# The opening of a hybrid attention layer: the inverse rms spread inside the value products, and the forget gates' turn, sum and store made steps of the planned list

## The chip, the cores and the metric

One core of a Trainium2 chip runs the whole layer. Its engines are TensorE (PE, matrix products into PSUM), VectorE (DVE), ScalarE (ACT), GpSimd (POOL) and SyncE (SP, which here issues all DMAs). Each takes its instructions in order from its own queue and waits on semaphores for the others. The metric is the device time of one execution in microseconds.

## What is computed

One layer with sequence 1024 and width 1024: a combined projection feeds two head groups, each of 8 heads of 64; their output is normalised and projected; then a cross-attention to 256 memory tokens and a squared-ReLU MLP follow. Only the start of it matters here:

```python
h = rmsnorm(x, g_mix_pre[l])
proj = h @ w_in[l]
...
f_logit = proj[..., o0:o0 + FOX_HEADS] + b_fgt[l]
...
# forgetting_attention
logf = jax.nn.log_sigmoid(f_logit.astype(jnp.float32))
c = jnp.cumsum(logf, axis=1).transpose(0, 2, 1)
...
logits = logits + c[:, :, q0:q1, None] - c[:, :, None, :q1]
```

So the first head group needs, beside q, k and v, the running sum c of the log forget gates over the sequence, for 8 heads.

## The kernel before

**Products.** Every float32 operand is split into a high part (a rounded copy, made by ScalarE) and a low part (the difference, made by VectorE or GpSimd), and `mm3` makes a product out of three passes: high by high, high by low, low by high (lines 174 to 176).

**Order.** The opening is written out by hand, lines 1422 to 1493: each engine gets its instructions in the order of the calls. Behind it `attention_phase` (line 1282) runs a planner, `Flow`. It takes steps for TensorE from seven streams by priority (values, turns of the probabilities, scores, side steps, two streams of row statistics, projections as filler). A step has a cost and a condition, and work that it leaves for the other engines goes into lists: "V" VectorE, "S" ScalarE, "G" GpSimd, "D" the DMA queue of SP, each with a start time, a cost and a level (lower goes first). The planner's clock starts at 0 with the phase, and `flow.free` says from when it takes an engine to be free. What it plans fixes the order of each queue; on the chip the semaphores decide the times.

**The opening.** x is there transposed, in two halves of 512 positions (`xf[0]`, `xf[1]`), each with 8 blocks of 128 features (kc). The values of the first group are made from x times the gain only, and scaled by the inverse rms afterwards, so they needn't wait for the norm:

- `plain_split(th, kc)` splits x times gain of half th into `hT[th]` (lines 1362 and 1363).
- `value_part(banks, th, w, kcs)` multiplies those kc into four PSUM banks. V is the first group of 256 value columns, with the 8 gate columns beside them, W the second 256. V uses the banks with tags "mm" and "s", W those with "tr" and "pv"; each tag has two buffers.
- `square(b)` sums the squares of a block of 128 positions (ScalarE, line 1369); `root(th)` makes the inverse rms of a half on GpSimd (lines 1375 and 1376) and four diagonal matrices from it on VectorE (line 1379).
- `values_out` copies the banks out, scaled by the inverse rms: ScalarE the high part (line 1416) and the gate column (line 1418), VectorE the low part (line 1419).
- `spread(th, d, tag)` multiplies a matrix of ones with the diagonals, which lays the inverse rms along the free axis (TensorE, line 1384), and copies it out (ScalarE, line 1386).
- `norm(th, kc)` scales x by gain and inverse rms in place (VectorE, line 1391), and `norm_split(th, kc)` splits the result into `hT[th]` again (lines 1396 and 1397), now for q and k.
- `forget_gates` gives the log sigmoid of the gates as a list of eleven small steps (`gparts`, lines 381 to 394, with an Exp, a Ln and an Exp on ScalarE, lines 387, 389 and 391), the turn (8 transposes on TensorE, line 399, and two copies, line 400), the running sum (a memset and a scan on VectorE, lines 403 and 404), and the store to DRAM (line 406). The bias tiles of the first head group are read back from there, spread over 128 partitions (line 433).
- `stock.split_now(2)` splits the first weights of q and k: ScalarE the high parts (line 311), GpSimd the low parts in halves (line 320).
- `bias_rows` prepares the relative biases of the second group (lines 223 to 228).

**The start of the phase.** The projections of the first pair of heads come as filler in the order q, k of the first half, q, k of the second, 8 steps of 0.681 us each, and their copies (lines 697 and 698 for q, 704 to 706 for k). The first scores (lines 495 and 496) need q and k of both halves and the bias tile. A side step needs a PSUM buffer of tag "tr".

Of the kernel before, what the change touches and what calls it, by code (L numbers as in the profile page):

```python
# [17 lines left out]
AF = mybir.ActivationFunctionType  # L18
# [4 lines left out]
P = 128  # L23
S = 1024
D = 1024
# [110 lines left out]
def build(ctx, tc, nc, out, t):  # L136
# [13 lines left out]
    def mm_tile(shape, name, tag="mm"):  # L150
        return psp.tile(shape, F32, tag=tag, bufs=2, name=name)
# [224 lines left out]
    def forget_gates():  # L376

        z, e, l, u = [p1.tile([P, TB, 8], F32, tag="fg", bufs=4, name=f"f{n}") for n in "zelu"]
        ea, la, ua = [p1.tile([8, S], F32, tag="klo", bufs=4, name=f"f{n}a") for n in "elu"]
        vec, act = nc.vector, nc.scalar  # L380
        calls = [lambda b=b: vec.tensor_add(z[:, b, :], fcol[:, b, :], bfgt) for b in range(TB)]
        rows_ = lambda: [calls.pop(0)() for _ in range(TB)]
        parts = [
            rows_,
            lambda: vec.tensor_scalar(l, z, -1.0, None, op0=ALU.mult),
            lambda: vec.tensor_tensor(l, l, z, op=ALU.min),
            lambda: act.activation(e, l, AF.Exp),
            lambda: vec.tensor_scalar(u, e, 1.0, None, op0=ALU.add),
            lambda: act.activation(l, u, AF.Ln),
            lambda: vec.scalar_tensor_tensor(e, u, 1.0, e, op0=ALU.subtract, op1=ALU.subtract),  # L390
            lambda: act.activation(u, l, AF.Exp, scale=-1.0),
            lambda: vec.tensor_tensor(e, e, u, op=ALU.mult),
            lambda: vec.tensor_sub(e, e, l),
            lambda: vec.scalar_tensor_tensor(e, z, 0.0, e, op0=ALU.min, op1=ALU.add)]

        def turn(g):
            tr = mm_tile([8, 4, P], f"ftr{g}", "s")
            for j in range(4):
                nc.tensor.transpose(tr[:, j, :], e[:, g * 4 + j, :], ident)
            act.activation(ea[:, g * HT:(g + 1) * HT], tr.rearrange("p a b -> p (a b)"), AF.Copy)  # L400

        def scan():
            vec.memset(ua, 0.0)
            vec.tensor_tensor_scan(la, ea, ua, 0.0, op0=ALU.add, op1=ALU.add)

        return parts, turn, scan, lambda: nc.sync.dma_start(cd, la)

    bias, qs, kd, kl, vs2, probs, trs, pvs = {}, {}, {}, {}, {}, {}, {}, {}
    heads = [(n, a) for n in range(8) for a in range(2)]
# [308 lines left out]

    def side_steps():

        for n in range(4, 8):
            for th in range(2):
                yield 0.436, lambda: there(("vt", n, th)) and free["tr"].ready()
                free["tr"].take()
                tr = mm_tile([P, 4, P], f"vtr{n}{th}", "tr")
                for b in range(4):
                    nc.tensor.transpose(tr[:, b, :], vt[n][:, th * HT + b * P:th * HT + (b + 1) * P], ident)
                src = tr.rearrange("p b (a d) -> p b a d", d=64)
                dst = vs2[n][th]

                def lo(at, src=src, dst=dst, key=("v", n, th)):
                    flow.put("V", at, 0.7, lambda: nc.vector.tensor_sub(
                        dst[:, :, :, 64:128], src, f(dst[:, :, :, 0:64])),
                        lambda end: (free["tr"].give(end), seen.__setitem__(key, end)), 1)

                flow.put("S", flow.end, 0.6, lambda src=src, dst=dst: nc.scalar.activation(
                    dst[:, :, :, 0:64], src, AF.Copy), lo, 1)
            free["u4"].give(flow.end)
        mT = Act("mT", NM)
        mem_in.append(mT)  # L740
        for k in range(0, KC, 2):
            yield 0.436, lambda: there("mem") and free["tr"].ready() and (k or free["u4"].ready(4))
            free["tr"].take()
            if k == 0:
                for _ in range(4):
                    free["u4"].take()
            tr = mm_tile([P, 2, 2, P], f"tr_mem{k}", "tr")
            for j in range(2):
                for q in range(2):
                    nc.tensor.transpose(tr[:, j, q, :], mem_in[q][:, (k + j) * P:(k + j + 1) * P], ident)  # L750
            src = tr.rearrange("p a q b -> p a (q b)")
            i, o = k // mT.per, k % mT.per
            dh, dl = mT.h[i][:, o:o + 2, :], mT.l[i][:, o:o + 2, :]

            def lo(at, src=src, dh=dh, dl=dl, k=k):
                flow.put("V", at, 0.7, lambda: nc.vector.tensor_sub(dl, src, f(dh)),
                         lambda end: (free["tr"].give(end), seen.__setitem__(("mT", k), end)), 1)

            flow.put("S", flow.end, 0.6, lambda src=src, dh=dh: nc.scalar.activation(dh, src, AF.Copy), lo, 1)
        for _ in range(2):  # L760
            free["raw"].give(flow.end)
# [534 lines left out]
    with tc.manual_schedule():  # L1296
# [76 lines left out]
        def root(th):  # L1373
            r = rall[:, th * 4:th * 4 + 4]
            nc.gpsimd.tensor_scalar(r, ssx[th], EPS, None, op0=ALU.add)
            nc.gpsimd.tensor_tensor(r, r, mhalf[:, 0:4], op=ALU.pow)
            d = p1.tile([P, 4, P], F32, tag="ph", bufs=2, name=f"diag{th}")
            for b in range(4):
                nc.vector.tensor_scalar(d[:, b, :], ident, r[:, b:b + 1], 1.0, op0=ALU.mult, op1=ALU.mult)
            return d  # L1380

        def spread(th, d, tag):
            ps = mm_tile([P, HT], f"rt{th}", tag)
            nc.tensor.matmul(ps, ones, d.rearrange("p a b -> p (a b)"), start=True, stop=True)
            r = p1.tile([P, HT], F32, tag="pl", bufs=2, name=f"rt{th}")
            nc.scalar.activation(r, ps, AF.Copy)
            rt.append(r)
# [16 lines left out]
        def value_part(banks, th, w, kcs):  # L1404
            for kc in kcs:
                for b in range(4):
                    c = slice(b * P, (b + 1) * P)
                    mm3(banks[b], hT[th].hi(kc, c), hT[th].lo(kc, c), *w[kc], kc == 0, kc == KC - 1)

        def values_out(g, th, banks):  # L1410
            for b in range(4):
                kb = th * 4 + b
                r = rall[:, kb:kb + 1]
                src = banks[b][:, 0:256].rearrange("p (h d) -> p h d", d=64)
                dh = vs[g][kb // 2][:, kb % 2, :, 0:64]
                nc.scalar.activation(dh, src, AF.Copy, scale=r)
                if g == 0:
                    nc.scalar.activation(fcol[:, kb, :], banks[b][:, 256:264], AF.Copy, scale=r)
                nc.vector.scalar_tensor_tensor(vs[g][kb // 2][:, kb % 2, :, 64:128], src, r, f(dh),
                                               op0=ALU.mult, op1=ALU.subtract)  # L1420
# [21 lines left out]
        nc.sync.dma_start(gcol, t["g_heads"])  # L1442
        stock.load(3)
        W = value_banks(1, 0)
        value_part(W, 0, w1, range(KC))
        d = root(0)
        values_out(0, 0, V)
        for kc in range(8):
            plain_split(1, kc)
        V = value_banks(0, 1)  # L1450
        value_part(V, 1, w0, range(4))
        values_out(1, 0, W)
        spread(0, d, "pv")
        value_part(V, 1, w0, range(4, 8))
        for b in range(4, 8):
            square(b)
        for kc in range(KC):
            norm(0, kc)
        d = root(1)
        for kc in range(KC):  # L1460
            norm_split(0, kc)
        W = value_banks(1, 1)
        value_part(W, 1, w1, range(3))
        gparts, turn, scan, gate_store = forget_gates()
        values_out(0, 1, V)
        spread(1, d, "s")
        value_part(W, 1, w1, range(3, 6))
        for call in gparts[:4]:
            call()
        stock.split_now(2)  # L1470
        for kc in range(4):
            norm(1, kc)
        for call in gparts[4:6]:
            call()
        for kc in range(4, KC):
            norm(1, kc)
        for call in gparts[6:]:
            call()
        for g in range(2):
            turn(g)  # L1480
        value_part(W, 1, w1, range(6, 8))
        for kc in range(4):
            norm_split(1, kc)
        scan()
        for kc in range(4, KC):
            norm_split(1, kc)
        values_out(1, 1, W)
        bias_rows(0)
        bias_rows(1)
        seen["gates"] = 11.0  # L1490
        flow.put("D", 7.0, 0.55, gate_store, None, -1)
        flow.put("D", 14.0, 0.55, lambda: nc.sync.dma_start(rd, rows[0]))
        flow.free.update(V=7.0, S=4.0)
        km, vmh, vml = attention_phase()
    p1s.close()

# [666 lines left out]
```

## Time and profile before

| | us |
|---|---|
| median of 3 runs | 1500.74 |
| lowest and highest run | 1495.99, 1501.56 |
| the profiled execution | 1498.95 |
| its span, first to last instruction | 1497.2 |

| engine | busy us | share of the span | instructions |
|---|---|---|---|
| TensorE | 1468.1 | 98% | 7564 |
| VectorE | 926.4 | 62% | 1599 |
| ScalarE | 794.6 | 53% | 1426 |
| GpSimd | 374.6 | 25% | 464 |

How to read the rows below. A row of a timeline has the start in us, the time it takes in us, the engine, the line of the kernel, the operation, what it writes and reads, the shape, and how many instructions are put together; in brackets stands how long the engine had been idle and what ended that. With several instructions, the time is from the first start to the last end. A row of the list of waits has who waited for whom, the total in us, how often, and the longest. A row of windows has the stretch, its length, the busy time of the engine, the granted TensorE clock (1.00 is full), the share of the DMA engines and GB/s.

### The profile page before, as it was taken

What the parts mean: (1) busy time and instruction counts of PE and PEld (TensorE: products, weight loads), DVE (VectorE), ACT (ScalarE), POOL (GpSimd) and SP (SyncE); (2) the same over time, 40 slices, a digit from 0 to 9 for tenths busy, and PEclk for the clock granted to TensorE, in tenths of its full rate; (3) what the DMA queues carried; (4) which work ended last, traced back from release to release, by engine and by line L of the source; (5) the groups of instructions that cost most, each with busy time, mean ns of one, the idle gap of its engine ahead of it and who ended that gap; (6) DMA issues with size and microseconds to landing.
All of it is one profiled execution on the core that took longest, in us unless ns stands there. A gap on an engine that the chain in (4) does not pass through costs nothing. (4 is left out here: it accounts for less than half of the span.)

```text
span 1497.2 us, 21427 instructions
## 1 busy us (share of the span) xinstructions
PE 1468.1 (98%) x7564; PEld 1250.3 (84%) x7564; DVE 926.4 (62%) x1599; ACT 794.6 (53%) x1426; POOL 374.6 (25%) x464
## 2 busy tenths in 40 slices
PE   8799999999999999999999999999999999999998
PEld 8678888888889988888888887888888888888886
DVE  4757766655565764884374577775545674646577
ACT  6537766666666763463354445555555553444442
POOL 1225444434333310431031422333323000000021
PEclk9899999999999999999999999999999999999999
DMA  8023222534225468461251356774345685436475
GB/s 325 29 86 103 68 77 66 157 94 137 75 76 153 140 249 300 173 236 58 76 178 57 103 182 201 259 247 145 139 161 176 231 343 203 140 121 212 174 253 197
DMA packets 95355, 239.54 MB, mean 160 GB/s; under 512 B 11896, under 2 KB 20224, under 8 KB 95248
## 3 DMA queue, kind: packets, MB, share of 16 engines
q1 hardware_dynamic: 95248, 238.18, 47.3%
q8 instruction: 59, 0.97, 0.3%
q14 instruction: 48, 0.39, 0.1%
HBM read 170.45 MB, written 59.30 MB: 153 GB/s over the span
## 5 line engine op out<-in xcount | busy, mean ns | idle before, releaser
L574 DVE TENSOR_TENSOR pl<-ptr,ph 128x512 fp32r<-128x512 f32 (+1 forms) x152 | 92.3, 615 | 63.1 <-ACT ph L577 62.6
L577 ACT ACTIVATE ph<-ptr 128x512 fp32r<-128x512 f32 (+1 forms) x152 | 79.6, 539 | 48.8 <-PE ptr L568 44.3
L1887 ACT ACTIVATE whif<-ra 128x1024 fp32r<-128x1024 f32 x37 | 39.2, 1060 | 122.7 <-PE fy L175 62.6
L1889 DVE TENSOR_TENSOR wlof<-ra,whif 128x1024 fp32r<-128x1024 f32 x37 | 45.3, 1225 | 91.3 <-ACT whif L1887 91.2
L2003 POOL TENSOR_SCALAR rf<-sf 128x1 f32<-128x1 f32 x8 | 8.2, 1030 | 326.3 <-ACT jf L1988 326.0
L174 PE MATMUL fx<-vhif,whif 128*128 128x512 f32 x168 | 65.4, 389 | 0.0
L176 PE MATMUL fx<-vhif,wlof 128*128 128x512 f32 x168 | 65.4, 389 | 0.0
L175 PE MATMUL fx<-vlof,whif 128*128 128x512 f32 x168 | 65.4, 389 | 0.0
L608 PE MATMUL pv<-pl,vs 128*128 128x256 f32 (+1 forms) x304 | 64.6, 294 | 0.2 <-DVE pl L574 0.2
L608 PEld LDWEIGHTS pv<-ph,vs 128*128 128x128 f32 x304 | 53.1, 189 | 7.3
L608 PE MATMUL pv<-ph,vs 128*128 128x256 f32 (+1 forms) x304 | 58.1, 272 | 0.0
L1777 POOL TENSOR_TENSOR sc<-wf,wf 128x512 f32<-128x512 f32 x14 | 21.9, 1565 | 143.6 <-DMA wf<-in_w_ff 87.7
L174 PE MATMUL k<-hT_hi,whik 128*128 128x512 f32 x128 | 52.2, 408 | 0.0
L174 PE MATMUL mq<-h2T_hi,whimq 128*128 128x512 f32 x128 | 51.6, 403 | 0.0
L174 PE MATMUL yw<-whiwo,yT_hi 128*128 128x512 f32 x128 | 50.8, 397 | 0.6 <-ACT yt L1047 0.6
L174 PE MATMUL q<-hT_hi,whiq 128*128 128x512 f32 x128 | 51.0, 399 | 0.4 <-DVE qs L698 0.4
L174 PE MATMUL ym<-whimo,oT_hi 128*128 128x512 f32 x128 | 50.3, 394 | 0.1
L175 PE MATMUL q<-hT_lo,whiq 128*128 128x512 f32 x128 | 50.1, 392 | 0.0
L175 PE MATMUL k<-hT_lo,whik 128*128 128x512 f32 x128 | 50.1, 391 | 0.0
L176 PE MATMUL k<-hT_hi,wlok 128*128 128x512 f32 x128 | 50.1, 391 | 0.0
L176 PE MATMUL q<-hT_hi,wloq 128*128 128x512 f32 x128 | 50.1, 391 | 0.0
L175 PE MATMUL mq<-h2T_lo,whimq 128*128 128x512 f32 x128 | 50.0, 391 | 0.0
(597 smaller groups left out, 4987.8 us busy)
## 6 DMA issues: line engine op xcount, KB each, us to landing
ra<-gd SPq DMA_DIRECT2D x56, 512.0 KB, 3.6
wg<-in_w_ff SPq DMA_DIRECT2D x56, 512.0 KB, 5.0
wf<-in_w_ff SPq DMA_DIRECT2D x38, 512.0 KB, 4.0
gd<-s SPq DMA_DIRECT2D x48, 256.0 KB, 2.1
wrawmq<-in_w_mq SPq DMA_DIRECT2D x16, 512.0 KB, 3.7
wrawmo<-in_w_mo SPq DMA_DIRECT2D x16, 512.0 KB, 3.9
gd<-u SPq DMA_DIRECT2D x32, 256.0 KB, 2.1
gd<-g SPq DMA_DIRECT2D x25, 256.0 KB, 2.5
```

Source lines behind the costliest of these rows:

```text
L174: nc.tensor.matmul(ps, lh, rh, start=start, stop=False, skip_group_check=more)
L175: nc.tensor.matmul(ps, lh, rl, start=False, stop=False, skip_group_check=more)
L176: nc.tensor.matmul(ps, ll, rh, start=False, stop=stop, skip_group_check=more)
L574: flow.put("V", at, 0.56 if dead else 0.7, lambda: nc.vector.tensor_sub(pl[:, live, :], tr[:, live, :], f(ph[:, live, :])), done)
L577: flow.put("S", flow.end, 0.49 if dead else 0.6, lambda ph=ph, tr=tr, live=live: nc.scalar.activation(ph[:, live, :], tr[:, live, :], AF.C ...
L608: nc.tensor.matmul(pv[:, q0:q0 + k1 - k0, :], v, x[:, k0:k1, :], start=c == 0 and m == 0, stop=c + 1 == len(steps) and m == 3, skip_group_ ...
L1777: eng.tensor_sub(sc[:, k1], r0[:, k0], r1[:, k0])
L1887: nc.scalar.activation(ah, ra, AF.Copy)
L1889: nc.vector.tensor_sub(al, ra, f(ah))
L2003: nc.gpsimd.tensor_scalar(r, ssf[b][:, 0:1], ssf[b][:, 1:2], EPS, op0=ALU.add, op1=ALU.add)
```

## The change

In the opening, W of the first half is interrupted after 5 of 8 kc for the spread of the first inverse rms, V of the second half after 5 of 8 for the spread of the second. Squares, norms and value copies are taken in among the splits. W of the second half runs through in one piece. The gates' small steps come in a new order among the norms and splits. The turn is parted into its transposes (`turn`) and its copies (`out`), uses the banks with tag "tr" in place of "s", and is a side step of the planner that may run when its clock is past 5.0; copies, scan and store follow as a chain of list items of level -1, and the time from which bias tiles may be read follows from that chain in place of the fixed 11.0. The planner is told that VectorE is free at 5.0 and ScalarE at 3.0, in place of 7.0 and 4.0.

```diff
@@ -393,17 +393,22 @@
             lambda: vec.tensor_sub(e, e, l),
             lambda: vec.scalar_tensor_tensor(e, z, 0.0, e, op0=ALU.min, op1=ALU.add)]
 
+        trs_ = []
+
         def turn(g):
-            tr = mm_tile([8, 4, P], f"ftr{g}", "s")
+            tr = mm_tile([8, 4, P], f"ftr{g}", "tr")
             for j in range(4):
                 nc.tensor.transpose(tr[:, j, :], e[:, g * 4 + j, :], ident)
-            act.activation(ea[:, g * HT:(g + 1) * HT], tr.rearrange("p a b -> p (a b)"), AF.Copy)
+            trs_.append(tr)
+
+        def out(g):
+            act.activation(ea[:, g * HT:(g + 1) * HT], trs_[g].rearrange("p a b -> p (a b)"), AF.Copy)
 
         def scan():
             vec.memset(ua, 0.0)
             vec.tensor_tensor_scan(la, ea, ua, 0.0, op0=ALU.add, op1=ALU.add)
 
-        return parts, turn, scan, lambda: nc.sync.dma_start(cd, la)
+        return parts, (turn, out), scan, lambda: nc.sync.dma_start(cd, la)
 
     bias, qs, kd, kl, vs2, probs, trs, pvs = {}, {}, {}, {}, {}, {}, {}, {}
     heads = [(n, a) for n in range(8) for a in range(2)]
@@ -718,6 +723,19 @@
 
     def side_steps():
 
+        yield 0.87, lambda: flow.now > 5.0 and free["tr"].ready(2)
+        turn, out = gate_turn
+        for g in range(2):
+            free["tr"].take()
+            turn(g)
+
+        def turned(at):
+            for _ in range(2):
+                free["tr"].give(at)
+            flow.chain(at, [("V", 3.2, gate_scan), ("D", 0.55, gate_store)],
+                       lambda at: seen.__setitem__("gates", at + 2.0), -1)
+
+        flow.chain(flow.end, [("S", 0.6, lambda: out(0)), ("S", 0.6, lambda: out(1))], turned, -1)
         for n in range(4, 8):
             for th in range(2):
                 yield 0.436, lambda: there(("vt", n, th)) and free["tr"].ready()
@@ -1442,55 +1460,62 @@
         nc.sync.dma_start(gcol, t["g_heads"])
         stock.load(3)
         W = value_banks(1, 0)
-        value_part(W, 0, w1, range(KC))
+        value_part(W, 0, w1, range(5))
         d = root(0)
         values_out(0, 0, V)
-        for kc in range(8):
+        spread(0, d, "s")
+        value_part(W, 0, w1, range(5, 8))
+        for kc in range(4):
             plain_split(1, kc)
         V = value_banks(0, 1)
         value_part(V, 1, w0, range(4))
+        for kc in range(4, 8):
+            plain_split(1, kc)
+        value_part(V, 1, w0, range(4, 5))
+        for b in range(4, 6):
+            square(b)
+        for kc in range(2):
+            norm(0, kc)
         values_out(1, 0, W)
-        spread(0, d, "pv")
-        value_part(V, 1, w0, range(4, 8))
-        for b in range(4, 8):
+        for b in range(6, 8):
             square(b)
-        for kc in range(KC):
+        for kc in range(2, 6):
             norm(0, kc)
         d = root(1)
+        spread(1, d, "pv")
+        value_part(V, 1, w0, range(5, 8))
+        for kc in range(6, KC):
+            norm(0, kc)
         for kc in range(KC):
             norm_split(0, kc)
         W = value_banks(1, 1)
-        value_part(W, 1, w1, range(3))
-        gparts, turn, scan, gate_store = forget_gates()
+        value_part(W, 1, w1, range(KC))
+        gparts, gate_turn, gate_scan, gate_store = forget_gates()
         values_out(0, 1, V)
-        spread(1, d, "s")
-        value_part(W, 1, w1, range(3, 6))
         for call in gparts[:4]:
             call()
         stock.split_now(2)
-        for kc in range(4):
+        for kc in range(3):
             norm(1, kc)
         for call in gparts[4:6]:
             call()
-        for kc in range(4, KC):
+        for kc in range(3, 6):
             norm(1, kc)
-        for call in gparts[6:]:
+        for call in gparts[6:8]:
             call()
-        for g in range(2):
-            turn(g)
-        value_part(W, 1, w1, range(6, 8))
-        for kc in range(4):
+        for kc in range(6, KC):
+            norm(1, kc)
+        for kc in range(2):
             norm_split(1, kc)
-        scan()
-        for kc in range(4, KC):
+        for call in gparts[8:]:
+            call()
+        for kc in range(2, KC):
             norm_split(1, kc)
         values_out(1, 1, W)
         bias_rows(0)
         bias_rows(1)
-        seen["gates"] = 11.0
-        flow.put("D", 7.0, 0.55, gate_store, None, -1)
         flow.put("D", 14.0, 0.55, lambda: nc.sync.dma_start(rd, rows[0]))
-        flow.free.update(V=7.0, S=4.0)
+        flow.free.update(V=5.0, S=3.0)
         km, vmh, vml = attention_phase()
     p1s.close()
 
```

## The prediction

> **What bounds the kernel now.** I read the page first, then the list of what TensorE waited for, then the granted clock in half-microsecond windows, then each engine's timeline over the first 115 us.
>
> ```profile
> span 1497.2 us, 21427 instructions
> PE ftr L399 <- DVE fe L394: 7.3, 1, 7.3
> PE rt L1384 <- DVE vs L1419: 3.8, 1, 3.8
> PE px L174 <- DVE u L1918: 1.1, 1, 1.1
> PE q L174 <- DVE qs L698: 0.4, 1, 0.4
> 100.00:150.00 50.00, 49.80 (x295) 43.32 (x294) 33.11 (x97) 32.11 (x68) 21.73 (x37) 1.00 0.30 85
> ...
> sum 1397.00, PE 1385.08 PEld 1175.30 DVE 866.74 ACT 740.46 POOL 351.78; mean PE 49.47 PEld 41.97 DVE 30.96 ACT 26.45 POOL 12.56
> ```
>
> The last two rows are windows: length, then busy time of TensorE, its weight loads, VectorE, ScalarE and GpSimd. From 100 us to the end TensorE idles 11.9 of 1397 us. It bounds the kernel, and what can be won lies in the opening, where two waits on VectorE take 7.3 and 3.8 us: the gates' turn (ftr) and the second spread of the inverse rms (rt). Each also costs clock:
>
> ```profile
> 52.50:53.00 0.50, 0.00 (x0) 0.61 0.00 0
> 59.00:59.50 0.50, 0.50 (x4) 0.56 0.00 0
> 66.00:66.50 0.50, 0.00 (x0) 0.77 0.90 352
> 73.00:73.50 0.50, 0.50 (x6) 0.91 0.00 0
> 33.64 0.29 PE L174 MATMUL v<-whiv,hT_hi 128*128 128x264 f32 x1
> 39.43 1.02 PE L1384 MATMUL rt<-diag,ones 128*128 128x512 f32 x2
> 54.36 2.08 PE L1384 MATMUL rt<-diag,ones 128*128 128x512 f32 x2 [3.78 <-DVE vs L1419]
> 69.46 1.87 PE L399 MATMUL ftr<-ident,fe 128*8 128x128 f32 x8 [7.34 <-DVE fe L394]
> 70.98 0.56 PE L174 MATMUL v<-whiv,hT_hi 128*128 128x256 f32 x1
> 74.87 0.40 PE L174 MATMUL q<-hT_hi,whiq 128*128 128x512 f32 x1
> 80.34 0.39 PE L174 MATMUL k<-hT_hi,whik 128*128 128x512 f32 x1
> 103.41 0.39 PE L495 MATMUL sf0g<-kd,qs 128*128 128x512 f32 x1
> ```
>
> The third column of the windows is the clock. Solved for the place of the step, it falls to half at 52.61 and 66.27 and rises at 59.44 and 73.09: a raster of 3.41 us (6.83 = 2 x 3.41). The first fall comes 2.0 us after the last product (54.36 - 3.78 = 50.58). The attention phase begins at 74.87; its first half projection (q) takes 5.47, and k begins at 80.34.
>
> **What the change does to TensorE's order.** A kc of four blocks is 12 products, and 48 take 39.43 - 33.64 = 5.79, so a kc is 1.45. Now W (frames 0 to 511) takes 5 kc, then the first spread, then 3 kc; V takes 5 kc, then the second spread, then 3 kc; W of the second half runs all 8 kc unbroken, and q follows with no turn ahead of it. The turn becomes a list step after the first 5 us of the phase, so it lands between q and k: the same 8 transposes, moved, not saved. Both old waits lose their place. The first spread, now earlier, finds its diagonals long done, so TensorE reaches the end of V's fifth kc at 33.64 + 1.0 (spread) + 5.79 + 1.45 = 41.9.
>
> **The second spread gets a new wait.** Its diagonals need the four squares, and ScalarE now stops for the first spread's copy before it splits:
>
> ```profile
> 25.24 5.04 ACT L1362 ACTIVATE hT_hi<-xf,gp 128x512 fp32r<-128x512 f32 x8
> 32.76 1.57 ACT L1416 ACTIVATE vs<-v,rall 128x256 fp32r<-128x256 f32 x4 [2.47 <-PE v L176]
> 40.48 0.60 ACT L1386 ACTIVATE rt<-rt 128x512 f32<-128x512 f32 x1 [6.16 <-PE rt L1384]
> 45.14 4.27 ACT L1396 ACTIVATE hT_hi<-xf 128x512 fp32r<-128x512 f32 x8
> 66.99 1.28 ACT L391 ACT_TABLE_LOAD   x1 [3.62 <-DVE fe L390]
> 47.44 0.88 DVE L1379 TENSOR_SCALAR diag<-ident,rall 128x128 f32<-128x128 f32 x4 [0.93 <-POOL rall L1376]
> ```
>
> The first spread starts at 33.64 - 3 x 1.45 = 29.3 in place of 39.43; its copy starts 1.05 behind it (40.48 - 39.43), 30.35, and frees ScalarE at 30.85. Then come eight splits (5.04), four squares (4.16, from 0.5 behind the copy at 40.48 to 45.14) and the value copies (1.57): 41.6. From the last square to the diagonals passed 47.44 - 45.14 = 2.3 (GpSimd's power among it), and they take 0.88: 44.8. TensorE waits from 41.9 to 44.8, 2.9 us, where it waited 3.8 later. Then spread, copy (45.85), split of the first half from 46.35. The norms and value differences that the change puts among the splits cost nothing: VectorE follows ScalarE's splits to about 37, has six norms and four value differences to do until the diagonals (by the rows below 4.0 + 1.6, so 43), and the last two norms (1.35) lie between the diagonals at 44.8 and the first split difference at 47.0. Without that cover they would add those 1.35 us to T0 below.
>
> **VectorE now sets the turn.** The turn's two banks are W's first two ("tr"), so the transposes wait for VectorE's second and first value difference of the second half (L1419), last but two in its opening.
>
> ```profile
> 41.12 5.39 DVE L1391 SCALAR_TENSOR_TENSOR xf<-xf,gp,rt 128x512 f32<-128x512 f32 x8 [6.19 <-ACT rt L1386]
> 54.61 0.69 DVE L381 TENSOR_TENSOR fz<-fcol,bfgt 128x8 f32<-128x8 f32 x8
> 57.10 4.80 DVE L1391 SCALAR_TENSOR_TENSOR xf<-xf,gp,rt 128x512 f32<-128x512 f32 x4 [1.30 <-ACT rt L1386]
> 61.82 1.25 DVE L388 TENSOR_SCALAR fu<-fe 128x64 f32<-128x64 f32 x1
> 62.99 3.78 DVE L1391 SCALAR_TENSOR_TENSOR xf<-xf,gp,rt 128x512 f32<-128x512 f32 x4
> 72.50 2.50 DVE L1397 TENSOR_TENSOR hT_lo<-xf,hT_hi 128x512 fp32r<-128x512 f32 x4 [3.19 <-ACT hT_hi L1396]
> 76.10 2.28 DVE L404 TENSOR_TENSOR_SCAN fla<-fea,fua 8x1024 f32<-8x1024 f32 x1
> 78.31 2.46 DVE L1397 TENSOR_TENSOR hT_lo<-xf,hT_hi 128x512 fp32r<-128x512 f32 x4
> 80.69 1.64 DVE L1419 SCALAR_TENSOR_TENSOR vs<-v,rall,vs 128x256 fp32r<-128x256 f32 x4
> 84.75 1.39 DVE L698 SCALAR_TENSOR_TENSOR qs<-q,qs 64x512 fp32r<-64x512 f32 x2
> 58.23 3.12 POOL L320 TENSOR_TENSOR wloq<-wrawq,whiq 128x512 fp32r<-128x512 f32 x2 [10.83 <-ACT whiq L311]
> 61.31 2.93 POOL L320 TENSOR_TENSOR wlok<-wrawk,whik 128x512 fp32r<-128x512 f32 x2
> 78.57 4.60 POOL L320 TENSOR_TENSOR wloq<-wrawq,whiq 128x512 fp32r<-128x512 f32 x2 [14.32 <-ACT whiq L311]
> 92.88 0.29 POOL L457 TENSOR_SCALAR_AFFINE_SELECT biasf<-biasf 128x128 f32<-128x128 f32 x1 [6.97 <-DMA biasf<-cd]
> ```
>
> First T0, where VectorE ends V's value differences: 47.0 (one split behind 46.35) + 8 x 0.61 (2.46 / 4) + 1.64 = 53.5. If the 2.9 us wait halves the clock, spread and copy come 1 us later (2.08 against 1.02): 54.4. The wait is longer than the 2.0 us that sufficed at 50.58, but the raster's phase is free; I take 53.9.
>
> The Trainium skill ("TensorE: Matmul & The Clock Gate", "What's actually happening") has the clock fall only after a whole idle window of about 3.4 us. By that rule 2.9 us is safe and T0 is 53.5; the trace had it fall 2.0 us into a wait, so the measurement decides and I keep the middle.
>
> From T0 to the second of W's value differences: gate sums 1.2 (54.61 to 57.10 - 1.30); eight norms of 0.67 (5.39 / 8), 5.4; five small gate operations 1.2; eight split differences 4.9; two value differences 0.8. To that I add GpSimd's weight splits: in the rows of 57.10 to 66.77 eight norms took 8.58 in place of 5.4 and a 0.2 us operation 1.25, so 4.2 us went to the four splits beside them (58.23 to 64.24). The same operations stand beside the same splits in the new order, so 4.2 stays. Last, the Exp: its table load of 1.28, its 0.26 and the first split of 0.6 follow the sixth norm, with two norms (1.35) as cover: 0.8 left. Sum 18.5. So the turn is free at 53.9 + 18.5 = 72.4, the first group 0.4 before.
>
> TensorE comes there at 45.8 + 4.35 + 11.6 + 5.47 = 67.2 (about 68.9 on a slow clock), so it waits 3 to 5 us, and restarts cold: transposes 70.98 - 69.46 = 1.5, k from 73.5, and as at 69.46 (3.6 us until 73.09) some 2.1 us of k at half speed, 1.05 lost. That puts k at an equivalent 74.6. Before, it was 80.34 plus the 0.4 us wait for qs: 80.7. **Gain 6.1 us.**
>
> **Moved at no cost, with its cover.** The scan (2.28, with its memset 3.2 as the list reckons it), the store and the bias loads follow the turn. VectorE ends the bias rows at 72.4 + 0.8 + 2.4 (82.33 to 84.75) = 75.6, does q's differences (1.39) and the scan by 80.2. From the scan's end to the mask of the first bias tile passed 92.88 - 78.38 = 14.5, with SP's queue between (weight loads, k's copies, bias loads, all behind the store): 94.7. The first score stood 22.7 behind k's equivalent start, now 97.3. Cover 2.6 us, where there were 10.2; if it is gone, TensorE waits one for one. The copies of k behind the store need k's own differences, at about 81, so they lose nothing. The list after that is dealt anew from the later gates; I take 0 for it, with -2 to +3 as bounds from the 11.9 us of idle that the dealing of today leaves.
>
> **Sum.** 1498.95 (the profiled execution, 1.75 above its span) - 6.1 = **1492.8**. That execution lies 1.8 below the median shown, inside the runs (1495.99 to 1501.56). Bounds of the terms: T0 53.5 to 54.4, restart 1 us either way, list -2 to +3: 1489.5 to 1497 for this case alone.
>
> **Rivals.**
> 1. VectorE isn't late: GpSimd loses the race instead. Beside the GpSimd row of 78.57 VectorE's four differences kept 0.61 each while that split ran long. Without the 4.2 us the turn is free at 68.2, TensorE waits 1 us or nothing, warm: k at 69.2, gain 11.5, 1487.5. Against it: the norms themselves, at 57.10 and 62.99, were the ones that slowed. [...]
> 2. No gain to measure: VectorE's waits for ScalarE (1.30 at 57.10, 3.19 at 72.50) move and don't vanish, since ScalarE's gate functions, weight splits and Exp keep their order. With both instead of my 0.8, 3.7 of the 6.1 are gone: 1496.5. Against it: the second spread's copy is now done before the gates start, and norms stand in front of the Exp.
> 3. Slower: the list. The planner takes VectorE to be free 5.0 us into the phase, and it is free some 13 later than q's start (75.6 against 61.7); before it said 7.0 and was 9.9 (84.75 - 74.87). TensorE runs its list in order, so a step dealt too early stalls it. Place: the first score of each of the 16 heads, behind bias, differences and copies. At the longest wait of today's later list (1.1, px) each: 16 x 1.1 = 17.6, 1510. It decides from 0.4 us a head (6.1 / 16). For it: the cover of 2.6. Against it: VectorE works 33 of 50 us there and catches up.
>
> **Chances.** Forecast 0.50, rival 1 0.15, rival 2 0.18, rival 3 0.17. 0.5% is about what a measurement of this kernel can tell from no change; against the median that is 7.5 us, 1493.2. Of the forecast 0.37 lies below it and 0.13 above; rival 1 adds 0.15 to faster, rival 2 its 0.18 to the same, rival 3 0.15 to slower and 0.02 to the same: 0.52, 0.33, 0.15. Range 1486 to 1506: rival 1 to most of the way to rival 3.
>
> **What would show it.** Right: a wait of about 3 us at rt with releaser diag, one of 3 to 5 at ftr with releaser vs (L1419), q's start near 62 to 63.5 and k's near 73.5, the first score near 97. Wrong: no wait at ftr (rival 1), DVE idle behind ACT of over 3 us between 54 and 72 (rival 2), new TensorE waits at s tiles after 95 us (rival 3).

## The result: 6.5 us faster, nearly all of it in the opening

The changed kernel took 1491.35 us in the median of 6 runs (1489.58 to 1493.0), the kernel before 1497.82 us of 6 (1495.99 to 1501.56): a ratio of 0.9951, with a 95% interval of 0.9936 to 0.9967. The profiled executions took 1491.91 and 1498.95 us. So it is faster, clear of the noise, by 0.49% (the ratio on record is that of the means; the medians alone give 0.9957). That is just at the half per cent that the prediction set as the bound: 1491.35 lies below its 1493.2, which was taken from the median of 1500.74 over three runs, but not below half a per cent under the later median, 1490.3.

The first line of the changed kernel's page (line numbers are now those of the changed file: spread 1402, diagonals 1397, value differences 1437, turn 401, norms 1409, splits 1414 and 1415, scan 409):

```profile
span 1490.1 us, 21429 instructions
```

The list of its TensorE waits (sum, count, longest):

```profile
PE ftr L401 <- DVE vs L1437: 3.3, 1, 3.3
PE rt L1402 <- DVE diag L1397: 2.7, 1, 2.7
PE px L174 <- DVE u L1943: 1.0, 1, 1.0
```

The two waits of 7.3 and 3.8 us are gone, and two others stand in their place: the second spread waits 2.7 us for its diagonals, the turn 3.3 us, no longer for the gates (fe) but for VectorE's value differences (vs), which free its banks.

TensorE's timeline (start, duration, and in brackets the wait ahead of it):

```profile
44.35 1.90 PE L1402 MATMUL rt<-diag,ones 128*128 128x512 f32 x2 [2.71 <-DVE diag L1397]
62.75 0.40 PE L174 MATMUL q<-hT_hi,whiq 128*128 128x512 f32 x1
71.73 1.82 PE L401 MATMUL ftr<-ident,fe 128*8 128x128 f32 x8 [3.34 <-DVE vs L1437]
73.19 0.78 PE L174 MATMUL k<-hT_hi,whik 128*128 128x512 f32 x1
96.69 0.39 PE L500 MATMUL sf0g<-kd,qs 128*128 128x512 f32 x1
```

q starts at 62.75 in place of 74.87, k at 73.19 in place of 80.34: of the 12 us that q is earlier, the turn with its wait, now between q and k, takes some 5 back. The first score stands at 96.69, where it stood at 103.41: 6.7 us of the span's 7.1.

Its windows, four of half a microsecond (length, TensorE's busy time, the clock) and the sum of those from 100 us to the end:

```profile
44.50:45.00 0.50, 0.50 (x1) 0.51 0.00 0
47.50:48.00 0.50, 0.50 (x5) 0.58 0.00 0
71.50:72.00 0.50, 0.27 (x2) 0.81 0.00 0
75.00:75.50 0.50, 0.50 (x3) 0.77 0.57 57
...
sum 1390.00, PE 1378.33 PEld 1170.94 DVE 867.04 ACT 739.97 POOL 353.94; mean PE 49.23 PEld 41.82 DVE 30.97 ACT 26.43 POOL 12.64
```

Both waits lower the clock to half, from 44.5 to 47.9 and from 71.8 to 75.2. Behind 100 us TensorE idles 1390.0 - 1378.3 = 11.7 us, against 11.9 before; from the first score to the end the two spans are alike, 1393.8 before and 1393.4 now.

The timeline of VectorE and GpSimd between the value differences of V and those of W, which was the working of the prediction's sum:

```profile
52.25 1.65 DVE L1437 SCALAR_TENSOR_TENSOR vs<-v,rall,vs 128x256 fp32r<-128x256 f32 x4
54.93 2.07 DVE L1409 SCALAR_TENSOR_TENSOR xf<-xf,gp,rt 128x512 f32<-128x512 f32 x3
57.02 5.18 DVE L1409 SCALAR_TENSOR_TENSOR xf<-xf,gp,rt 128x512 f32<-128x512 f32 x3
62.13 1.31 DVE L390 SCALAR_TENSOR_TENSOR fe<-fu,fe 128x64 f32<-128x64 f32 x1
65.62 1.29 DVE L1415 TENSOR_TENSOR hT_lo<-xf,hT_hi 128x512 fp32r<-128x512 f32 x2 [0.86 <-ACT hT_hi L1414]
71.10 1.65 DVE L1437 SCALAR_TENSOR_TENSOR vs<-v,rall,vs 128x256 fp32r<-128x256 f32 x4
77.77 2.28 DVE L409 TENSOR_TENSOR_SCAN fla<-fea,fua 8x1024 f32<-8x1024 f32 x1
56.33 3.62 POOL L320 TENSOR_TENSOR wloq<-wrawq,whiq 128x512 fp32r<-128x512 f32 x2 [13.04 <-ACT whiq L311]
59.91 3.44 POOL L320 TENSOR_TENSOR wlok<-wrawk,whik 128x512 fp32r<-128x512 f32 x2
87.89 0.29 POOL L462 TENSOR_SCALAR_AFFINE_SELECT biasf<-biasf 128x128 f32<-128x128 f32 x1 [10.95 <-DMA biasf<-cd]
```

Three norms alone take 2.07; the three beside GpSimd's splits take 5.18, and the small gate operation behind them 1.31.

### The profile page after: what moved, and what is told of

Read it like the earlier page. It is cut to its first block, busy times and chain, and to the rows that moved or that the text cites. A ratio compares the mean times of both kernels' runs of the same rounds, so it can differ in the third digit from the quotient of the medians.

```text
span 1490.1 us, 21429 instructions
## 1 busy us (share of the span) xinstructions
PE 1466.0 (98%) x7564; PEld 1249.1 (84%) x7564; DVE 928.4 (62%) x1599; ACT 795.2 (53%) x1426; POOL 375.7 (25%) x464
```

## The experiments

Each kernel is the changed one, or the one before where it is said, with one edit. Times are medians; the ratio on record is to the kernel before on the same chip at the same time (median 1497.73 us for the first four, 1498.47 for the last four; it isn't the quotient of the two medians). "Opening" is, in the one profiled execution, the time from the first product of W (at 22.13 in the kernel before, 21.87 in the changed one, 19.80 to 23.19 in the others) to the first score. It leaves out how long the start took, which differs between executions of one kernel, and "rest" is from there to the end. Both are single executions: "planner told as before" has the changed kernel's order up to the first score and yet an opening 2.4 us shorter, because its clock fell at other places, so that much of an opening can be the execution and not the edit.

| kernel | median | ratio, 95% interval | opening | rest |
|---|---|---|---|---|
| before | 1497.82 | | 81.3 | 1393.8 |
| changed | 1491.35 | 0.9951, 0.9936 to 0.9967 | 74.8 | 1393.4 |
| gates alone | 1493.96 | 0.9974, 0.9964 to 0.9983 | 77.6 | 1392.1 |
| spread alone | 1496.66 | 0.9984, 0.9974 to 0.9993 | 79.2 | 1396.0 |
| turn in s banks | 1488.08 | 0.9933, 0.9919 to 0.9946 | 73.8 | 1393.3 |
| kept warm | 1487.47 | 0.9929, 0.9917 to 0.9942 | 72.4 | 1391.2 |
| splits early | 1486.79 | 0.9926, 0.9913 to 0.9938 | 71.5 | 1391.5 |
| s banks and splits early | 1486.65 | 0.9928, 0.9916 to 0.9941 | 70.3 | 1396.0 |
| all | 1486.22 | 0.9929, 0.9916 to 0.9942 | 68.8 | 1393.5 |
| planner told as before | 1493.01 | 0.9965, 0.9953 to 0.9977 | 72.4 | 1396.2 |

**The turn in other banks.**

```diff
-            tr = mm_tile([8, 4, P], f"ftr{g}", "tr")
+            tr = mm_tile([8, 4, P], f"ftr{g}", "s")
...
-        yield 0.87, lambda: flow.now > 5.0 and free["tr"].ready(2)
+        yield 0.87, lambda: flow.now > 5.0 and free["s"].ready(2)
```

> The changed kernel, but the turn takes the two banks with tag s, free since 53.9 us of its trace, in place of the tr banks that wait for VectorE's value differences. Theory (VectorE's queue sets the turn through the tr banks): the wait of 3.3 us at ftr goes, since the last gate operation ends at 67.6 and TensorE comes at 68.4; no clock is lost there; k starts near 69.3 in place of 73.2. The next thing late is then the bank of q, whose differences VectorE gives at 75.9 behind the bias rows, while k's first half ends near 74.8: a new wait of about 1 us. Sum: about 3.5 to 4.5 us faster than the changed kernel, 1487. Rival (the turn waits for the gates' values themselves, not for the banks): the wait at ftr stays at 3 us and the time at 1491.4. Rival (the gain is given back behind it, since VectorE is as late as before): below 1 us faster.

Its timeline at the turn and at its one new wait:

```profile
67.78 1.03 PE L401 MATMUL ftr<-ident,fe 128*8 128x128 f32 x8
76.63 0.47 PE L174 MATMUL q<-hT_hi,whiq 128*128 128x512 f32 x1 [2.34 <-DVE qs L703]
75.79 0.69 DVE L703 SCALAR_TENSOR_TENSOR qs<-q,qs 64x512 fp32r<-64x512 f32 x1 [0.66 <-ACT qs L702]
```

Its windows at the rise behind the first wait and at a second fall, with the clock third:

```profile
47.00:47.50 0.50, 0.50 (x5) 0.90 0.00 0
77.50:78.00 0.50, 0.50 (x4) 0.82 0.99 98
```

The wait at the turn is gone with the banks, so it was the banks and not the gates that held it. It was 3.3 us faster than the changed kernel by the medians, a little under what was expected. The next thing late was the one named, q's bank, but with 2.3 us in place of 1, because the second of q's differences came behind a copy of ScalarE. The clock then fell at 77.8, after the wait had ended, and cost more of what had been won: the profiled opening is only 1.0 us shorter. The profiled execution was the slowest of the five (1490.34) with the lowest mean clock (0.996, the other four 0.998), so this fall need not be in the others, and its opening may understate what the edit gave.

**Kept warm.** Products that nobody reads, in the two waits:

```diff
         def spread(th, d, tag):
             ps = mm_tile([P, HT], f"rt{th}", tag)
+            for _ in range(20 if th else 0):
+                nc.tensor.matmul(ps[:, 0:256], hT[1].hi(0, slice(0, P)), w1[0][0], start=True, stop=True)
...
         turn, out = gate_turn
+        idle = mm_tile([P, HT], "idle", "s")
+        for _ in range(10):
+            nc.tensor.matmul(idle, stock.w["q", 0][0][:, 0, :], hT[0].hi(0), start=True, stop=True)
```

> The changed kernel with products that nobody reads in its two waits of the opening: 20 of 256 columns ahead of the second spread, 10 of 512 columns ahead of the turn. Theory (the waits cost clock beside their length): the granted clock stays at 1.00 from 15 us on; the second spread's copy comes 0.9 us earlier, so T0 and the turn do as well; the eight transposes take 0.9 in place of 1.46 and k loses no 0.9 us. Sum 2.3 us faster than the changed kernel, 1489. Rival (VectorE sets the end and the clock is hidden): only what lies behind the turn, 1.4 us or less. Rival (the skill's page says that the clock falls only after a whole idle window; then the added products change nothing at the first wait): T0 stays at 53.8.

Its TensorE waits:

```profile
PE ftr L401 <- DVE vs L1442: 1.9, 1, 1.9
PE rt L1407 <- DVE diag L1400: 0.2, 1, 0.2
```

and its timeline at the turn:

```profile
71.77 1.03 PE L401 MATMUL ftr<-ident,fe 128*8 128x128 f32 x8 [1.89 <-DVE vs L1442]
72.56 0.48 PE L174 MATMUL k<-hT_hi,whik 128*128 128x512 f32 x1
```

The clock is granted in full in every window from 16 to 94 us. The transposes take 72.56 - 71.77 = 0.8, where they took 1.5, and the opening is 2.4 us shorter, as forecast. W began 0.9 later than in the changed kernel (22.77 against 21.87) and the turn started at the same time, so the bank came 0.9 earlier by its own measure: the first wait's clock was on VectorE's path too. T0, the end of V's value differences, says the same. On the profile's clock it is 53.95 and so looks unmoved, as the rival had it, but it lies 31.2 us behind W's first product, where it was 32.0; with the planner told as before, where the clock fell only behind the spread, it is 31.2 as well. The medians differ by 3.9; the rest of the kernel, which this edit doesn't touch, was 2.2 shorter in this execution.

**The weight splits earlier.** ScalarE and GpSimd split the first weights of q and k behind the second root:

```diff
         d = root(1)
+        late = small.tile([P, 1], F32, tag="rstd", bufs=8, name="late")
+        nc.gpsimd.tensor_copy(late, d[:, 3, 0:1])
+        stock.split_now(2)
         spread(1, d, "pv")
...
-        stock.split_now(2)
         for kc in range(3):
             norm(1, kc)
```

> The changed kernel with the first weight splits of q and k moved from among the gates to behind the second root, where ScalarE and GpSimd are idle; a one-column copy on GpSimd holds them behind the diagonals. Theory (GpSimd's four splits beside VectorE's norms cost VectorE 4 us and so hold the turn): the eight norms of the second half take 0.67 each throughout, W's value differences end 4 us earlier, the wait at ftr of 3.3 us shrinks to nothing and its clock loss goes: 4 to 5 us faster than the changed kernel, 1487. Rival (the two engines share whatever they meet on: the splits now slow the split differences of the first half instead): T0 3 to 4 us later, no gain or 1 us.

Its timeline, VectorE first, then GpSimd and TensorE:

```profile
45.42 7.66 DVE L1415 TENSOR_TENSOR hT_lo<-xf,hT_hi 128x512 fp32r<-128x512 f32 x8 [1.70 <-ACT hT_hi L1414]
53.00 1.65 DVE L1437 SCALAR_TENSOR_TENSOR vs<-v,rall,vs 128x256 fp32r<-128x256 f32 x4
57.76 2.07 DVE L1409 SCALAR_TENSOR_TENSOR xf<-xf,gp,rt 128x512 f32<-128x512 f32 x3
67.62 1.66 DVE L1437 SCALAR_TENSOR_TENSOR vs<-v,rall,vs 128x256 fp32r<-128x256 f32 x4
46.08 3.45 POOL L320 TENSOR_TENSOR wlok<-wrawk,whik 128x512 fp32r<-128x512 f32 x2
68.25 1.03 PE L401 MATMUL ftr<-ident,fe 128*8 128x128 f32 x8 [1.69 <-DVE vs L1437]
```

From the end of V's differences to the end of W's it is now 69.28 - 54.65 = 14.6, where it was 72.75 - 53.90 = 18.85: the splits had cost 4.2 us, as the sum had it. It was GpSimd's part of them: in the changed kernel ScalarE's two high parts (55.21 to 57.20) ran beside the three norms that took 2.07, and slowed nothing. But eight split differences of the first half, now beside the splits, take 7.66 in place of 4.91 in the changed kernel, so 2.8 of it are lost again ahead. Both theories were partly right; the wait at the turn shrank to 1.7 us, no longer enough to lower the clock, and the opening became 3.3 us shorter. By the medians this gave 4.6.

**Each part alone.** From the kernel before, first the gates' move:

```diff
-        value_part(W, 1, w1, range(3, 6))
+        value_part(W, 1, w1, range(3, KC))
...
-        for g in range(2):
-            turn(g)
-        value_part(W, 1, w1, range(6, 8))
...
-        scan()
...
+        yield 0.87, lambda: flow.now > 5.0 and free["tr"].ready(2)
```

> The kernel before with the second part of the change alone: turn, sum and store of the gates as list steps, the planner's two numbers, but the opening's order of spreads, squares and splits as it was. Theory: the wait of 3.8 us at the second spread stays, W's rest runs unbroken, q starts near 64 us; VectorE, which still waits 1.3 us for the spread's copy but no longer holds for the scan and the turn, gives W's first two differences near 75, so the turn waits some 5 us there and k starts near 76.5: some 3 us slower than the changed kernel and 4 faster than before, 1494. Rival (the spread carries the gain): within 1.5 us of before, 1497. Rival (the gates' move carries it all): 1491.4.

Then the spread, with W's first 6 kc, the turn (banks s) and 2 kc, and the scan as before:

```diff
-        value_part(W, 1, w1, range(3))
+        value_part(W, 1, w1, range(6))
         gparts, turn, scan, gate_store = forget_gates()
         values_out(0, 1, V)
-        spread(1, d, "s")
-        value_part(W, 1, w1, range(3, 6))
```

> The kernel before with the first part of the change alone: spreads, squares, norms and copies in the new order, but the turn in the opening (banks s, behind 6 kc of W), the scan among the last split differences, the store and the planner's numbers as before. Theory (the spread's wait is only traded for another, and it is the turn's move that lets W run): TensorE ends the 6 kc near 59.5 and waits for the last gate operation until 67.6, some 8 us; it restarts cold, q starts near 73, k near 78.5 with no wait behind it: 2 to 2.5 us faster than before, 1495.5. Rival (the two parts add up: the whole change gave 6.5, the gates alone 3.8): 2.7 faster, 1495, which this run can't tell apart from the theory by time, but by the wait at ftr. Rival (the spread carries the gain): 1491.4.

TensorE's timeline with the gates alone:

```profile
72.26 1.87 PE L401 MATMUL ftr<-ident,fe 128*8 128x128 f32 x8 [4.48 <-DVE vs L1437]
73.78 0.78 PE L174 MATMUL k<-hT_hi,whik 128*128 128x512 f32 x1
```

Its waits with the spread alone:

```profile
PE ftr L399 <- DVE fe L394: 7.9, 1, 7.9
PE rt L1384 <- DVE diag L1379: 2.7, 1, 2.7
```

and k's start there:

```profile
76.53 0.39 PE L174 MATMUL k<-hT_hi,whik 128*128 128x512 f32 x1
```

The gates alone gave 3.8 us (1497.73 - 1493.96), the spread alone 1.8 (1498.47 - 1496.66), both together 6.5: the openings, 3.7 and 2.1 against 6.5, say the same. So the parts nearly add up, and the larger one is the gates'. With the spread alone the second wait of 3.8 shrinks to 2.7, but the turn's grows from 7.3 to 7.9. k's start agrees with the expectation once the early start is taken off (W began 2.1 us before that of the changed kernel: 78.6). With the gates alone it doesn't quite: by the same measure (W began 1.65 us earlier) k came at 75.4, where 76.5 was expected.

**Two edits, and all that helped.** The turn in the s banks with the splits early; then with the unread products ahead of the second spread as well, and the bias rows as list items:

```diff
-        bias_rows(1)
-        flow.put("D", 14.0, 0.55, lambda: nc.sync.dma_start(rd, rows[0]))
+        flow.chain(14.0, [("V", 2.0, lambda: bias_rows(1)), ("D", 0.55, lambda: nc.sync.dma_start(rd, rows[0]))])
```

> The changed kernel with two edits together: the turn in the s banks and the weight splits early. Theory (both cut the same wait at ftr, so they don't add up): no wait at ftr, k starts near 67.3, and q's differences near 73 come just in time behind bias rows; 1 to 1.5 us faster than the early splits alone, 1485.5. Rival (they add up): 1483.5. Rival (q's bank takes the wait over in full): 1486.8.

> The changed kernel with all that helped: the turn in the s banks, the weight splits early, the unread products ahead of the second spread, and the bias rows (2.0 us of VectorE) as list items at 14.0 in place of the end of the opening, so that q's differences come 2 us earlier. Theory: granted clock 1.00 from 15 us on, no wait of over 0.5 us from 16 to 100 us but the second spread's, k near 66, first score near 88.5: 2 us faster than the two edits without them, 1483.5. Rival (ScalarE and the list hold the rest): 1485.5.

TensorE's waits of the last of them, from 0 to 110 us:

```profile
PE v L174 <- ACT hT_hi L1380: 5.3, 1, 5.3
PE q L174 <- DVE qs L703: 0.4, 1, 0.4
PE rt L1404 <- DVE diag L1397: 0.2, 1, 0.2
```

and VectorE's split differences in its timeline:

```profile
45.26 8.21 DVE L1417 TENSOR_TENSOR hT_lo<-xf,hT_hi 128x512 fp32r<-128x512 f32 x8 [1.04 <-ACT hT_hi L1416]
```

TensorE now waits for nothing of note between its first product and the first score, and the opening is 6 us shorter than the changed kernel's. The time doesn't follow: 1486.65 and 1486.22, where the theories had 1485.5 and 1483.5, and ratios as with the early splits alone (0.9926). So both theories missed (the first one's rival, q's bank with the whole wait, is near by its 1486.8 alone: q waited 0.4 us), and not by the opening: in the last kernel k came at 66.04 and the first score at 89.32, near the 66 and 88.5 expected. In the two profiles the rest took 4.5 and 2.0 us more than the 1391.5 with the early splits alone; what made it longer isn't shown. The first of these figures sets the slowest of six executions (1489.61) against the fastest of five (1484.88), so part of it may be the execution alone. So the best of these kernels are alike, at about 5 us below the changed one, and which of them is the fastest stays open.

**What the planner is told.**

```diff
-        flow.free.update(V=5.0, S=3.0)
+        flow.free.update(V=7.0, S=4.0)
```

> The changed kernel with the planner told 7.0 and 4.0 again in place of 5.0 and 3.0; the order of the list differs in some places. Theory (what the planner believes of the first microseconds hardly counts, the queues themselves do): within 1 us of the changed kernel, 1491.4, the wait at ftr as before. Rival (dealing the list anew costs or gives microseconds behind the opening): 3 us or more away from it, with waits that differ behind 95 us.

One of its waits, its timeline at the second spread and at the turn, and its windows:

```profile
PE px L174 <- DVE u L1943: 2.2, 1, 2.2
```

```profile
45.67 1.10 PE L1402 MATMUL rt<-diag,ones 128*128 128x512 f32 x2 [2.71 <-DVE diag L1397]
72.25 0.92 PE L401 MATMUL ftr<-ident,fe 128*8 128x128 f32 x7 [2.62 <-DVE vs L1437]
```

```profile
72.50:73.00 0.50, 0.50 (x7) 0.39 (x5) 0.50 (x2) 0.50 (x2) 0.50 (x1) 1.00 0.00 0
910.00:920.00 10.00, 7.82 (x29) 6.08 (x28) 3.78 (x6) 3.19 (x4) 5.12 (x4) 0.86 0.94 322
```

1.7 us slower by the median, but the intervals overlap (0.9953 to 0.9977 against 0.9936 to 0.9967): between the two theories, and inconclusive. The opening didn't suffer, and its 72.4 is the clock's doing: behind the same wait of 2.71 us the clock fell only at 46.7, so the spread took 1.10 us in place of 1.90, VectorE came 0.8 us earlier by W's start, the wait at the turn shrank to 2.6, and there the clock didn't fall at all. The rest took 2.8 us more. The one wait that grew is that at px, 2.2 us in place of 1.0, at 910 to 920 us; the clock fell there too (0.86 in that window, where the changed kernel has 1.00 and TensorE busy for 8.97 of the 10 us), so some 1.2 us of the 2.8 have a place in the code far behind the opening, and for the others no place is shown.

## Why the prediction was right, point by point

It said 1492.8, a gain of 6.1 on the profiled execution; that gained 7.0, and the medians 6.5.

- **TensorE's order and the new first wait.** 2.9 us were worked out for the second spread, behind diagonals at 44.8; 2.7 were measured, from 41.6 to 44.35, with the diagonals as releaser. The gain and its limit come from the same place: ScalarE holds still for the first spread's copy, and the squares come late by that.
- **T0.** 53.5 without and 54.4 with a fallen clock, 53.9 taken; measured 52.25 + 1.65 = 53.90. That it fits to the hundredth is luck. The clock fell, as the row of 50.58 had suggested, so the sum's own figure was 54.4; the diagonals were done at 44.2 in place of 44.8 (0.26 of it because W began earlier), and that made up for it. By the rule of the Trainium skill ("TensorE: Matmul & The Clock Gate", "What's actually happening"), a whole idle window, 2.7 us would have been safe; the windows at 44.50 and 47.50 show that they weren't, and the kept-warm kernel shows that it cost.
- **From T0 to the turn.** 18.5 were summed, 71.10 + 0.82 - 53.90 = 18.0 measured. The split's share of 4.2 was settled by moving it, 18.85 against 14.6 to the end of the differences. The wait for the Exp was put at 0.8 and was 0.86.
- **The turn.** A wait of 3 to 5 us, released by the value differences: 3.3, and so it was. k was expected at 73.5 and started at 73.19.
- **The moved scan, store and loads.** Their cover was put at 2.6 us and was much larger. The first bias tile was masked at 88.2 and first needed at 98.2, so 10 us. The step that failed is the 14.5 us from scan to mask, carried over from before: now it is 87.89 - 80.05 = 7.8. Before, SP sent two weight loads out between store and bias loads, at 83.20 and 85.93, each right behind GpSimd's splits of 78.57 to 85.91; in the new order the last such load is ahead of the store, and the bias loads follow at 83.48, as the rows of SP's timeline below show. From store to bias loads it is now 3.4 us, where it was 7.9, so this is 4.5 of the 6.7 us; the other 2.2 lie between the bias loads' issue and the mask (6.6 before, 4.4 now), and their cause is open. The copies of k lost nothing, as said: k's differences came at 81.13. As the term entered the sum with 0, nothing changed in the time. First SP before, then after:

```profile
83.20 0.34 SPq L298 DMA_DIRECT2D wrawk<-in_w_qk  x1
85.93 0.33 SPq L298 DMA_DIRECT2D wrawq<-in_w_qk  x1
```

```profile
76.97 0.33 SPq L298 DMA_DIRECT2D wrawq<-in_w_qk  x1
80.08 0.30 SPq L411 DMA_DIRECT2D cd<-fla  x1
83.48 1.03 SPq L438 DMA_DIRECT2D biasf<-cd  x2
```

- **The list.** 0 with -2 to +3; 0.4 us were gained behind the first score, in one execution each.
- **The rivals.** The first (GpSimd loses the race) is wrong: the norms slowed as before, and the split differences, whose row at 78.31 spoke for it, slowed as well when the splits came beside them (7.66 and 8.21 for eight, in place of 4.91). Which engine yields isn't fixed by the operation; what made the difference at 78.31 stays open. The second (the waits for ScalarE only move) is wrong: of 4.5 us at two places, 0.86 was left at one, and TensorE's new waits were those of the sum. The third (the list) doesn't hold for this change, but its size is no fancy: the rest differs by up to 5 us between these kernels, in single executions, so that the kernel's share and the execution's aren't told apart.
- **What was uncertain.** Of the 0.9 us by which the profiled execution beat the sum, 0.6 lies ahead of the first score (97.3 expected, 96.69 measured; W began 0.26 earlier) and the rest behind it, where the list had been entered with 0.

## What to carry to other kernels

When work is drawn out of an engine's way at one place, look at once for what holds the buffers of the work that moves up: here the turn no longer waited for its data, but 3.3 us for the banks that VectorE's queue still had to empty. Cost a wait with the clock that it may lower, not by its length alone; a wait of 2.7 us cost about another microsecond on the path. And where three engines are nearly in step, a second edit on the same wait brings little: the best of two alone and both together came out alike.

## What the runs showed of the hardware

- **The clock's raster decides, not the wait alone.** In the kernel before and in the changed one, rises and falls lie a multiple of 3.41 us apart. With the turn in the s banks the boundaries fall at 74.40 and 77.82 (counted from the rise at 47.10), 2.2 us of that window were idle, and the clock fell at its end, 1.2 us after work had begun again. With the planner told as before, a longer wait of 2.6 us (69.63 to 72.25) was cut by a boundary at 70.63 into 1.0 and 1.6, and the clock stayed. So some 2.0 us idle within one window were enough (the kernel before, 50.58 to the boundary at 52.61), and 1.6 were not. And the same wait of 2.71 us at the second spread cost VectorE 0.8 us or nothing, as the boundary fell before the spread's end or behind it.
- **The start differs too, by the same raster.** Nothing is changed ahead of W, yet it began anywhere from 19.80 to 23.19 us in the ten profiles. The first product came at 5.2 to 5.4 us in nine of them (6.1 in the tenth); what differs is when a product takes 0.28 us and no longer 0.42: from 8.8 us on at the earliest (splits early), 13.9 in the changed kernel, 15.1 in the one before, 16.1 with the planner told as before. The column of the clock doesn't show this step, it reads 1.00 there. But counted back from the clock's first later rise in steps of 3.41, the raster has boundaries at 8.8, 13.8, 15.1 and 16.0 in these four; in seven of the eight profiles that have a rise the step lies within 0.1 us of a boundary, and in the eighth (gates alone, 8.7) the boundary falls into a wait of TensorE. So the phase of the raster, which differs between executions, sets when full speed begins. That it makes up most of the 3.4 us between the first products of W, and so a good part of the spread between executions of one kernel, is argued, since no run sets that phase; waits for data play a part too (the spread alone reached full speed at 11.2 and yet began W first).
- **GpSimd's splits hold VectorE up by 0.6 to 1.05 us each, but not always.** Four of them added 4.2 us to VectorE's queue among norms, and 2.4 to 3.3 among eight split differences (7.26, 7.66 and 8.21 in the three kernels that have them there, 4.91 without). The copy of the bias rows (L228) took 1.38 us beside the next splits in the changed kernel, and 0.41 in the last one, where it ran behind them. Against that stands the prediction's row of 78.31, where VectorE's four differences kept 0.61 each and the split ran long.
